# A two-block transformer layer on one core: GpSimd's tile arithmetic moved to VectorE, gates stored as tanh, and the modulation's products moved between stages

## The chip, the core and the metric

The program runs on one core of a Trainium2 chip. The time is the device time of one execution in microseconds (us), median over runs; the profile shows one such execution. The core's engines are named as in the profile: PE is TensorE's matmul queue, PEld its weight loads, DVE is VectorE, ACT ScalarE, POOL GpSimd, SP SyncE, which here issues the DMA transfers. Each engine runs its own instructions in order and waits for the others by semaphores.

## What is computed

256 tokens of width 2048 go through two blocks, all in float32. The first mixes by an S5 state space model and a gated DeltaNet, the second by sliding-window attention and gated linear attention (GLA); each ends in a gated convolutional FFN, and the second is modulated by a vector c. Cut to what the change touches:

```python
h = rmsnorm(x, mix_norm_w)
u, qkv, z, b_raw, a_raw, g_s5, g_dn = split(h @ w_in)
glu_a, glu_b = split(s5_branch(u) @ s5_glu_w)
br_s5 = glu_a * sigmoid(glu_b)
br_dn = deltanet_branch(qkv, z, b_raw, a_raw) @ dn_proj_w
x = x + (sigmoid(g_s5) * br_s5 + sigmoid(g_dn) * br_dn) @ w_out
h = rmsnorm(x, ffn_norm_w)
act, val = split(causal_dwconv(h @ ffn_up, ffn_conv_w))      # 3 taps
x = rmsnorm(x + (silu(act) * val) @ ffn_down, final_norm_w)
mod = silu(c) @ w_mod + b_mod                                # 2048 x 12288
sh1, sc1, g1, sh2, sc2, g2 = split(mod)
h = rms_norm(x) * (1 + sc1) + sh1
merged = sigmoid(g_a) * (attention(h) @ w_br_a) + sigmoid(g_b) * (gla(h) @ w_br_b)
x = x + g1 * rms_norm(merged @ w_out2)
x = x + g2 * rms_norm(conv_ffn(rms_norm(x) * (1 + sc2) + sh2))
```

## The kernel before

**Jobs and units.** Each product with a weight matrix is a job; they run in the order u, ba, q, k, v, z, gs, glu, gdn, dnp, wout, up1a, dw1a, up1b, dw1b, then qa, ka, va, gk, qb, kb, vb, og, ga, gb, wba, wbb, wout2, up2a, dw2a, up2b, dw2b. A job is cut into groups of output columns. Its weights come in chunks of 1 MB by SP's queue into three buffers `raw` (`fetch`). Half a chunk is a unit: ACT rounds it to `hi` (L413), and `split` subtracts, `lo = raw - hi`, by `tt` (L271): the low part, 128x1024, usually on DVE. Four pairs hi, lo can be alive. `run` then issues for each k-tile a matmul with hi over 512 columns (the two parts of the activations) and one with lo over 256 (L451, L452), or three for jobs whose result has tokens on the partitions (L457 to L459).

**The evacuation.** Two PSUM tiles `main` alternate. When a group's last k-tile is issued, a generator `ev_...` empties it, a step between two k-tiles of the next group: `halves` copies one half by ACT (L469) and adds on DVE (`ev<-main,evlo`). In up1a and up1b (`ev_up`) follow a product with R, the row of inverse norms, on POOL; a scaling by ACT (`tmp<-ev,pv`); four multiply-adds of the convolution on DVE (L278, 255 and 254 columns); Silu on ACT; the product of the two halves on POOL (`tmp<-tmp`); and its split by ACT and DVE (`act1a`). The gates gs, gdn, ga and gb are evacuated by a tanh and an addition on POOL (L275) and stored to DRAM until the branch outputs are merged.

**Background work.** S5, DeltaNet, attention and GLA are generators too, stepped beside the main products; S5 must be finished before glu begins, DeltaNet before dnp. Their small matmuls go to the tiles `bank`. A scheduler then fixes each engine's final order.

**What POOL does before.** The low part of every fourth unit in gs, glu, ga, gb, up1a and up1b, and of the first four of qa and up2a (`on_pool`); the products with R; the gates' additions; the merges; part of S5's, DeltaNet's, attention's and GLA's arithmetic; the first squares of x, which are summed on PE.

**The modulation.** w_mod's 96 chunks of 1 MB share the `raw` buffers. DVE multiplies each with silu(c) and sums along the row (L404, the GEMV). `plan` places one after every second or third chunk of the jobs that `MOD_EVERY` names (L333):

```python
if (ci >= 4 or nm != "up1a") and mods < 96 and since >= self.MOD_EVERY.get(nm, 1 << 30):
    self.units.append((len(self.chunks), None, 0, 0))
```

Of the kernel before, what the change touches and what calls it, by code (L numbers as in the profile page):

```python
# [13 lines left out]
P = 128  # L14
L = 256
# [27 lines left out]
def job_list():  # L43
    """Groups name the 128-column tiles of each packed matrix."""
# [75 lines left out]
def tile_columns(src, w):  # L120
    """The matrix [k, tiles * 128] that the groups index, from the reference's one."""
# [117 lines left out]
def pieces(v, n):  # L239
    """v as n floats of 12 bits each and one of the rest."""  # L240
# [9 lines left out]
# ------------------------------------------------------------------ kernel  # L250
# [6 lines left out]
class Kern:  # L257
# [11 lines left out]
    # ---- small wrappers  # L269
# [31 lines left out]
    # ---- background  # L301
# [55 lines left out]
    def fetch(self, upto, part=None):  # L357
        """Loads chunks up to one; with part, only the next so many columns of one."""
# [28 lines left out]
    POOL_EVERY = {"gs": 4, "glu": 4, "ga": 4, "gb": 4, "up1a": 4, "up1b": 4}  # L387

    def on_pool(self, u):
        """Whether GpSimd makes the low parts of a unit."""  # L390
        j = self.chunks[self.units[u][0]][0].name
        n = u - self.job_start[j]
        e = self.POOL_EVERY.get(j, 0)
        return j in ("qa", "up2a") and n < 4 or e and n % e == 1

    def split(self, upto):
        while self.split_at < min(upto, len(self.units)):
# [16 lines left out]
            eng = self.G if self.on_pool(u) else self.V  # L414
            self.tt(lo, r, hi.bitcast(F32), A.subtract, eng)
# [3 lines left out]
    def run(self, name, rhs, evac, ready=None):  # L419
        """rhs(k): the [128, 512] split tile of k; evac(g, psum) makes the generator that empties a group."""  # L420
# [44 lines left out]
    def halves(self, ps, nf=2, out=None):  # L465
        """The sum of a group's two halves, [128, nf, 256]."""
# [26 lines left out]
    def exp(self, out, x, n, t):  # L493
        """out = e ** x, to float32's accuracy; x is overwritten."""
# [13 lines left out]
    def turns(self, th, tmp, hi=None):  # L508
        """th (overwritten) in turns modulo 1 as a list [e] in [-.5, .5], or (hi, lo) with hi of 16 bits."""
# [29 lines left out]
    def token_rows(self, bank, col, acc, n=1):  # L539
        """Sums over partitions of acc [128, 256] into bank[:, col:col+2], a token on each partition."""  # L540
# [3 lines left out]
    def spread(self, bank, at, r, dg):  # L544
        """bank[:, at:at+256] = r (a token on each partition) along every row."""
# [5 lines left out]
    # ---- set-up  # L551
# [34 lines left out]
    def split_scaled(self, k, x, w):  # L586
        """xs[k] = the two parts of x * w (w a column)."""
# [4 lines left out]
    def split_into(self, dst, x, scale=1.0):  # L592
        """dst [128, 512] = the two parts of x * scale."""
# [7 lines left out]
    def rsqrt_mean(self, out, sums):  # L601
        """out [128, 2] = (mean of squares + eps) ** -0.5 from the sums of groups [128, 2, n]."""
# [5 lines left out]
    def row_scale(self, r):  # L608
        """self.R = r (a token on each partition, [128, 2]) along rows."""
# [4 lines left out]
    def square_sums(self, x, sums, quick=False):  # L614
        """sums [128, 2] = sums of squares of x [128, 2, n]; quick: by two engines."""
# [8 lines left out]
    def tiles(self, name, g):  # L624
        """The columns of a group."""
# [3 lines left out]
    def to_features(self, i, x):  # L629
        """Columns 256 i to 256 i + 255 of x [128 tokens, 2, n], a column on each partition."""  # L630
# [9 lines left out]
    # ---- block 1  # L640
    def block1(self):
# [9 lines left out]
        # the functions' table is loaded before the data is there  # L651
# [58 lines left out]
        self.run("gs", self.xrhs, lambda g, ps: self.ev_gate(self.d_gs, g, ps, 1.0))  # L710
# [4 lines left out]
        self.run("gdn", self.xrhs, lambda g, ps: self.ev_gate(self.d_gdn, g, ps, 2.0))  # L715
# [24 lines left out]
    def ev_u(self, g, ps):  # L740
        raw = self.halves(ps)
        yield
        if g == 0:
            # written first so that these loads come after the first weights
# [7 lines left out]
        self.tt(u, eo(raw), eo(self.rbc(2)), A.mult, self.G)  # L752
# [56 lines left out]
    def ev_glu(self, f, ps):  # L809
# [8 lines left out]
        self.tt(raw[:, 0], raw[:, 0], gl, A.mult, self.G)  # L818
# [11 lines left out]
    def ev_dnp(self, g, ps):  # L830
# [8 lines left out]
        yield  # L839
# [17 lines left out]
    # ---- the S5 branch  # L857
    def s5_task(self):
# [3 lines left out]
        # two steps of the recurrence at a time: x[2m+1] = a^2 x[2m-1] + (a B u[2m] + B u[2m+1])  # L862
# [79 lines left out]
        self.ts(c1, c1, -1.0, A.mult, 0.0, A.add, G)  # L942

        def cmul(o, o2, x, y, p, q, op, op2):
            """o = x p op y q, o2 = y p op2 x q."""
            self.tt(o, x, p, A.mult, G)
            self.tt(t3, y, q, A.mult)
            yield
            self.tt(o, o, t3, op, G)
            yield  # L950
            self.tt(o2, y, p, A.mult, G)
            self.tt(t3, x, q, A.mult)
            yield
            self.tt(o2, o2, t3, op2, G)
# [28 lines left out]
        def tables(j):  # L983
# [20 lines left out]
        for j in range(8):  # L1004
# [21 lines left out]
            self.tt(t1, t1, t2, A.add, G)  # L1026
# [875 lines left out]
```

## Time and profile before

| | |
|---|---|
| runs | 3260.02, 3258.59, 3263.13 us, median 3260.02 |
| profiled execution | span 3257.4 us; no separate time of it is given |
| front: u to gdn | 7.4 to 697.7 us |
| k, v | 146.8 to 211.3, 211.3 to 277.1 |
| wout | 743.0 to 835.6, 189 GB/s |
| up1a, up1b | 835.6 to 1113.6, 1241.6 to 1513.3 |
| og, ga, gb | from 1944.8, 2033.6, 2153.8, to 2259.3 |
| wba, wbb | 2259.3 to 2304.6, 2304.6 to 2393.4 |
| wout2 | 2393.4 to 2504.0, 190 GB/s |
| up2a, up2b | 2504.0 to 2751.6, 2875.1 to 3119.2 |

A stage begins with its job's first main matmul and ends with the next job's. In the row of a stage the busy time of PE, PEld, DVE, ACT and POOL stand in this order, then the granted clock of PE as a share of full speed, the busy share of the DMA engines and what they moved. In a row of a group stand line, engine, operation, output<-inputs, shapes and count, then its busy time in us, the mean duration of one in ns, and the engine's idle time just before, with what ended it. In a row of waits stands who waited for whom, the total in us, how often, and the longest.

### The profile page before, as it was taken

How to read it: one execution, taken by the hardware profiler on the slowest of the kernel's cores; microseconds unless marked ns; L12 is line 12 of the kernel's file. 1: busy time of each engine (PE TensorE's matmuls, PEld its weight loads, DVE VectorE, ACT ScalarE, POOL GpSimd, SP SyncE). 2: the span in 40 equal slices, each digit the busy share in tenths (PEclk: the TensorE clock that was granted, in tenths of full speed). 3: DMA queues.
4: the chain of work that ended last, by engine and by line, in shares of the span. 5: the costliest groups of instructions: out<-in, count | busy, mean ns of one | idle time of the engine just before them, and what ended most of it. 6: DMA issues, size and time to landing. Idle time of an engine off the chain costs nothing.

```text
span 3257.4 us, 46596 instructions
## 1 busy us (share of the span) xinstructions
PE 3099.1 (95%) x18220; PEld 2665.1 (82%) x18220; DVE 2300.3 (71%) x3043; ACT 1589.3 (49%) x2276; POOL 872.4 (27%) x491
## 2 busy tenths in 40 slices
PE   7889999999988999989989999999997999999998
PEld 6767789888877788777878898778887888898887
DVE  8999775666777767777667767887566666456655
ACT  4445543554444434444444544645444655445543
POOL 3665452231355403554020000332211111001101
PEclk9999999999999999999999999999998999999999
DMA  6334464665566677666756668666755555555553
GB/s 242 132 127 141 174 227 156 237 235 207 220 240 244 236 264 263 254 245 241 256 188 241 228 247 317 240 248 247 278 194 184 206 192 184 187 198 186 190 192 131
DMA packets 130829, 701.73 MB, mean 215 GB/s; under 512 B 20200, under 2 KB 33176, under 8 KB 53680
## 3 DMA queue, kind: packets, MB, share of 16 engines
q1 hardware_dynamic: 130608, 698.75, 60.0%
q8 instruction: 143, 2.34, 0.3%
q14 instruction: 78, 0.64, 0.1%
HBM read 674.26 MB, written 24.44 MB: 214 GB/s over the span
## 4 chain that ended last, share of the span: by engine, by line
PE 44%; DVE 3%; DMA 1%; issue 1%; ACT 1%; DVEq 0%; SPq 0%; ACTq 0%
PE main L451 19%; PE main L452 10%; PE main L457 5%; PE main L458 5%; PE main L459 5%; DMA raw<-in_wmod 1%; DVE lo L271 1%; DVE X L271 0%; PE bank L634 0%; DVE big L278 0%; ACT L282 0%; DVE raw L404 0%; DVE asm L275 0%; ACT X L282 0%; PE bank L1663 0%
## 5 line engine op out<-in xcount | busy, mean ns | idle before, releaser
L451 PE MATMUL main<-xs,hi 128*128 128x512 f32 x5440 | 1922.5, 396 | 17.2 <-ACT hi L413 9.2
L271 DVE TENSOR_TENSOR lo<-raw,hi 128x1024 fp32r<-128x1024 f32 x940 | 1201.3, 1282 | 628.7 <-ACT hi L413 626.1
L452 PE MATMUL main<-xs,lo 128*128 128x256 f32 x5440 | 1541.4, 284 | 56.4 <-DVE lo L271 38.7
L413 ACT CAST hi<-raw 128x1024 fp32r<-128x1024 f32 (+1 forms) x1024 | 1063.2, 1043 | 1000.7 <-PE main L451 560.5
L451 PEld LDWEIGHTS main<-xs,hi 128*128 128x128 f32 x5440 | 1030.5, 190 | 250.3 <-DVE xs L278 10.7
L452 PEld LDWEIGHTS main<-xs,lo 128*128 128x128 f32 x5440 | 1031.5, 190 | 83.6 <-DVE lo L271 49.8
L271 POOL TENSOR_TENSOR tmp<-tmp 128x256 f32<-128x256 f32 (+1 forms) x93 | 187.6, 2017 | 647.0 <-ACT tmp L282 646.6
L271 POOL TENSOR_TENSOR lo<-raw,hi 128x1024 fp32r<-128x1024 f32 x84 | 211.5, 2518 | 534.3 <-ACT hi L413 447.5
L404 DVE CUSTOM_DVE_ANT_0 raw<-raw,sc 128x2048 f32<-128x2048 f32 x96 | 242.4, 2525 | 42.2 <-DMA raw<-in_wmod 41.7
L271 POOL TENSOR_TENSOR ev<-ev,R 128x512 f32<-128x512 f32 x76 | 140.4, 1847 | 282.6 <-DVE ev L271 282.6
L278 DVE SCALAR_TENSOR_TENSOR tmp<-ev,pv,tmp 128x255 f32<-128x255 f32 (+1 forms) x352 | 162.7, 524 | 74.7 <-ACT tmp L282 74.7
L282 ACT ACTIVATE tmp<-ev,pv 128x256 f32<-128x256 f32 x176 | 88.1, 548 | 119.5 <-POOL ev L271 119.3
L271 DVE TENSOR_TENSOR ev<-main,evlo 128x512 f32<-128x512 f32 (+1 forms) x190 | 129.0, 679 | 14.3 <-ACT evlo L469 10.5
L457 PE MATMUL main<-hi,xs 128*128 128x256 f32 (+1 forms) x448 | 138.6, 309 | 0.0
L458 PE MATMUL main<-lo,xs 128*128 128x256 f32 (+1 forms) x448 | 137.4, 307 | 0.0
L459 PE MATMUL main<-hi,xs 128*128 128x256 f32 (+1 forms) x448 | 137.1, 306 | 0.0
L469 ACT COPY evlo<-main 128x512 f32<-128x512 f32 (+1 forms) x203 | 117.0, 576 | 13.7 <-PE main L452 13.7
L271 POOL TENSOR_TENSOR ev<-ev,tmp 128x512 f32<-128x512 f32 (+1 forms) x48 | 59.4, 1238 | 200.1 <-DVE ev L271 107.0
L451 PE MATMUL main<-ysp,hi 128*128 128x512 f32 x256 | 92.0, 400 | 0.4 <-DVE ev L271 0.4
L457 PEld LDWEIGHTS main<-hi,xs 128*128 128x128 f32 x448 | 84.1, 188 | 6.0 <-issue 1.7
L458 PEld LDWEIGHTS main<-lo,xs 128*128 128x128 f32 x448 | 84.3, 188 | 4.9 <-issue 0.7
L459 PEld LDWEIGHTS main<-hi,xs 128*128 128x128 f32 x448 | 84.5, 189 | 4.7
(336 smaller groups left out, 3863.0 us busy)
## 6 DMA issues: line engine op xcount, KB each, us to landing
raw<-in_w_in SPq DMA_DIRECT2D x164, 1024.0 KB, 4.9
raw<-in_wmod SPq DMA_DIRECT2D x96, 1024.0 KB, 5.1
raw<-in_ffn_up SPq DMA_DIRECT2D x88, 1024.0 KB, 5.0
raw<-in_w_up SPq DMA_DIRECT2D x88, 1024.0 KB, 4.8
raw<-in_ffn_down SPq DMA_DIRECT2D x38, 1024.0 KB, 5.0
raw<-in_w_down SPq DMA_DIRECT2D x38, 1024.0 KB, 4.8
raw<-in_w_out SPq DMA_DIRECT2D x32, 1024.0 KB, 4.8
raw<-in_s_glu_w SPq DMA_DIRECT2D x16, 1024.0 KB, 4.9
```

Of the source, the lines that this page charges most:

```text
L271: (eng or self.V).tensor_tensor(out=out, in0=a, in1=b, op=op)
L278: self.V.scalar_tensor_tensor(out=out, in0=a, scalar=s, in1=b, op0=op0, op1=op1)
L282: self.S.activation(out, a, f, bias=bias, scale=scale, **kw)
L404: self.V.tensor_tensor_reduce(r, r, self.sc, 1.0, 0.0, A.mult, A.add, self.mod[:, m:m + 1])
L413: self.S.copy(hi, r)
L451: T.matmul(cur[:, f, :], hi[:, s], x, start=first, stop=False)
L452: T.matmul(cur[:, f, 0:L], lo[:, s], x[:, 0:L], start=False, stop=last)
L457: T.matmul(cur[:, h, :w], xh, hi[:, s], start=first, stop=False)
L458: T.matmul(cur[:, h, :w], xh, lo[:, s], start=False, stop=False)
L459: T.matmul(cur[:, h, :w], xl, hi[:, s], start=False, stop=last)
L469: self.S.copy(lo[:, :nf], ps[:, :nf, L:])
```

## The change

All arithmetic on tiles leaves GpSimd. The low parts are all DVE's, `on_pool` and `POOL_EVERY` are gone, and every `tt` or `ts` that named GpSimd is now on DVE. The gates are stored as tanh, without the addition; whoever uses them computes (t + 1) * x in one instruction. The sums of the first squares come from a token-major copy of x, loaded at the start, by two squares with a sum on ACT. The GEMVs per job change from (up1a 20, dw1a 8, up1b 22, dw1b 8, qb 4, kb 4, vb 8, og 8, ga 8, gb 6) to (wout 5, up1a 4, dw1a 12, up1b 4, dw1b 12, qb 4, kb 4, vb 8, og 8, ga 8, gb 8, wba 4, wbb 8, wout2 7). The last three modulation vectors are formed after wout2.

```diff
-    MOD_EVERY = {"up1a": 2, "dw1a": 3, "up1b": 2, "dw1b": 3, "qb": 2, ... "wba": 2, "wbb": 2}
+    MOD_EVERY = {"wout": 2, "up1a": 11, "dw1a": 2, "up1b": 11, "dw1b": 2, "qb": 2, ... "wbb": 2, "wout2": 2}
-                if (ci >= 4 or nm != "up1a") and mods < 96 and ...
+                if (ci >= 6 or nm != "wout") and mods < 96 and ...
-    POOL_EVERY = {"gs": 4, "glu": 4, "ga": 4, "gb": 4, "up1a": 4, "up1b": 4}
-            eng = self.G if self.on_pool(u) else self.V
-            self.tt(lo, r, hi.bitcast(F32), A.subtract, eng)
+            self.tt(lo, r, hi.bitcast(F32), A.subtract)
...
-        for i in range(4):
-            self.tt(sq[:, i > 0], x[:, 4 * i:4 * i + 4], x[:, 4 * i:4 * i + 4], A.mult, G)
...
+        xt = self.ys32.rearrange("p (h n) -> p h n", h=2)
+        self.dma(xt, ap["xt"])
+        for h in range(2):
+            self.act(self.tmp[:, 0:2048], xt[:, h], AF.Square, accum=self.ss[0][:, h, 0:1])
...
     def ev_gate(self, dst, g, ps):
-        self.tt(raw, raw, self.rbc(2), A.mult, self.G)
+        self.tt(raw, raw, self.rbc(2), A.mult)
         self.act(raw, raw, AF.Tanh, scale=0.5)
-        self.ts(raw, raw, c, A.mult, c, A.add, self.G)
...
     def ev_dnp(self, g, ps):
-        self.tt(raw, raw, t[:, 0], A.mult, self.G)
-        self.tt(raw, raw, t[:, 1], A.add, self.G)
+        self.stt(raw, t[:, 0], 1.0, raw, A.add, A.mult)
+        self.stt(raw, raw, 2.0, t[:, 1], A.mult, A.add)
...
     def ev_up(self, b, f, i, act, done, ps):
-            self.tt(raw, raw, self.rbc(2), A.mult, self.G)
+            self.tt(raw, raw, self.rbc(2), A.mult)
...
-        self.tt(cv[:, 0], cv[:, 0], cv[:, 1], A.mult, self.G)
+        self.tt(cv[:, 0], cv[:, 0], cv[:, 1], A.mult)
...
+        self.run("wout2", self.xrhs, self.ev_wout2)
+        self.flush()
         sh2, sc2 = self.modulation(3), self.modulation(4)
         self.tt(gw2, self.modulation(5), self.pv("ffnpost", 0, 16), A.mult)
         self.stt(a2, sc2, 1.0, self.pv("ffnpre", 0, 16), A.add, A.mult)
-        self.run("wout2", self.xrhs, self.ev_wout2)
-        self.flush()
```

The same kind of edit, an engine left out of the call, is made in S5 (`cmul`, `roundn`, the sums of the scan), in DeltaNet, in attention's rotation, in GLA, in `ev_qkv`, `ev_z`, `ev_glu`, `ev_wba`, `ev_wbb`, `ev_down`, and in the residual additions after wout2 and at the end. POOL's queue falls from 359 instructions of the program's order to 15.

What the diff doesn't show is the order that results. DVE in the middle of up1a, one group of columns before:

```order
L271 TENSOR_TENSOR lo<-raw,hi 128x1024
L271 TENSOR_TENSOR ev<-main,evlo 128x512
L271 TENSOR_TENSOR lo<-raw,hi 128x1024
L278 SCALAR_TENSOR_TENSOR tmp<-ev,pv,tmp 128x255 x2
L278 SCALAR_TENSOR_TENSOR tmp<-ev,pv,tmp 128x254 x2
L271 TENSOR_TENSOR lo<-raw,hi 128x1024
L404 ISA raw,mod<-raw,sc 128x2048
L404 ISA mod 128x1
L271 TENSOR_TENSOR act1a<-tmp,act1a 128x256
```

and one group now:

```order
L271 TENSOR_TENSOR ev<-main,evlo 128x512
L271 TENSOR_TENSOR ev<-ev,R 128x512
L271 TENSOR_TENSOR lo<-raw,hi 128x1024
L278 SCALAR_TENSOR_TENSOR tmp<-ev,pv,tmp 128x255 x2
L278 SCALAR_TENSOR_TENSOR tmp<-ev,pv,tmp 128x254 x2
L271 TENSOR_TENSOR lo<-raw,hi 128x1024
L271 TENSOR_TENSOR tmp<-tmp 128x256
L271 TENSOR_TENSOR lo<-raw,hi 128x1024
L271 TENSOR_TENSOR act1a<-tmp,act1a 128x256
L271 TENSOR_TENSOR lo<-raw,hi 128x1024
```

Before, the evacuation's sum is followed by a low part and the multiply-adds, with the products by R and `tmp<-tmp` in POOL's queue and a GEMV in almost every group. Now both products stand in DVE's order, one low part stands between each two steps, and a GEMV stands in one group of five or six.

PE where S5's last matmuls (`bank`, L1053 and L1056, in the changed kernel L1029 and L1032) stand among the main products of gs, before:

```order
L451 MATMUL main<-xs,hi 128x512
L1053 MATMUL bank_66<-big,ysp 32x127 x4
L452 MATMUL main<-xs,lo 128x256
L451 MATMUL main<-xs,hi 128x512
L1053 MATMUL bank_66<-big,ysp 32x127 x4
L1056 MATMUL bank_66<-big,ysp 32x128 x16
L452 MATMUL main<-xs,lo 128x256
```

and now:

```order
L442 MATMUL main<-xs,lo 128x256
L441 MATMUL main<-xs,hi 128x512
L1029 MATMUL bank_66<-big,ysp 32x127 x4
L442 MATMUL main<-xs,lo 128x256
L1029 MATMUL bank_66<-big,ysp 32x127 x4
L1032 MATMUL bank_66<-big,ysp 32x128 x16
L441 MATMUL main<-xs,hi 128x512
```

Before, these rows come after 59 of the 512 main matmuls of gs; now after 448. S5 is spread over the stages q to gs, and DeltaNet's doubling levels, which stood among glu's products, stand among gdn's.

## Rows read from the trace of the kernel before

**Rows 1.** The page, part 1: busy time of each engine.

```profile
PE 3099.1 (95%) x18220; PEld 2665.1 (82%) x18220; DVE 2300.3 (71%) x3043; ACT 1589.3 (49%) x2276; POOL 872.4 (27%) x491
```

**Rows 2.** Waits in up1a: us in total, times, longest.

```profile
ACT act1a L282 <- POOL tmp L271: 60.6, 20, 4.0
...
ACT tmp L282 <- POOL ev L271: 53.8, 19, 3.7
...
DVE tmp L278 <- ACT tmp L282: 36.9, 20, 2.9
...
PE main L452 <- DVE lo L271: 12.8, 12, 1.6
```

**Rows 3.** Busy time by stage (window, length, engines, PEclk, DMA share, GB/s).

```profile
7.40:697.70 690.30, 643.94 (x4210) 540.11 (x4211) 548.37 (x875) 332.39 (x466) 294.98 (x182) 0.97 0.52 182
146.80:211.30 64.50, 58.90 (x434) 47.41 (x433) 61.07 (x112) 32.63 (x44) 39.13 (x21) 0.97 0.39 135
211.30:277.10 65.80, 60.27 (x434) 47.76 (x433) 64.20 (x109) 35.40 (x48) 39.75 (x20) 0.97 0.38 132
835.60:1113.60 278.00, 253.31 (x1418) 215.58 (x1417) 216.35 (x248) 130.22 (x194) 150.84 (x62) 1.00 0.65 242
1241.60:1513.30 271.70, 251.60 (x1410) 215.78 (x1409) 211.44 (x236) 129.89 (x188) 139.93 (x62) 0.99 0.69 251
1944.80:2033.60 88.80, 88.80 (x515) 78.19 (x514) 65.56 (x64) 41.22 (x47) 2.42 (x1) 1.00 0.83 309
2033.60:2153.80 120.20, 110.18 (x611) 92.38 (x610) 98.59 (x129) 70.21 (x108) 38.28 (x24) 0.97 0.68 249
2153.80:2259.30 105.50, 103.22 (x610) 89.24 (x609) 84.50 (x139) 56.20 (x90) 34.38 (x23) 1.00 0.65 221
2259.30:2304.60 45.30, 45.30 (x259) 39.33 (x258) 28.34 (x30) 21.66 (x27) 10.31 (x8) 1.00 0.88 331
2304.60:2393.40 88.80, 88.80 (x515) 78.20 (x514) 50.52 (x51) 42.09 (x54) 24.89 (x15) 1.00 0.71 242
2504.00:2751.60 247.60, 247.60 (x1431) 218.13 (x1430) 171.28 (x243) 146.32 (x214) 30.14 (x21) 1.00 0.55 194
2875.10:3119.20 244.10, 244.10 (x1411) 214.86 (x1410) 163.50 (x215) 137.22 (x194) 30.69 (x21) 1.00 0.55 192
```

**Rows 4.** DVE's groups by line, front (busy us, mean ns | idle before).

```profile
L271 DVE TENSOR_TENSOR lo<-raw,hi 128x1024 fp32r<-128x1024 f32 x165 | 221.2, 1345 | 89.2 <-ACT hi L413 88.8 <-issue 0.2
...
L278 DVE SCALAR_TENSOR_TENSOR big<-ev,pv,big 128x255 f32<-128x255 f32 x24 | 25.9, 1111 | 0.4 <-ACT big L282 0.4
...
L271 DVE TENSOR_TENSOR big<-big 128x512 f32<-128x512 f32 x24 | 15.9, 672 | 0.0
...
L278 DVE SCALAR_TENSOR_TENSOR xs<-big,pv,xs 128x256 fp32r<-128x256 f32 x14 | 15.4, 1153 | 0.6 <-ACT xs L282 0.6
```

**Rows 5.** The same view, og.

```profile
L271 DVE TENSOR_TENSOR lo<-raw,hi 128x1024 fp32r<-128x1024 f32 x32 | 39.1, 1223 | 21.1 <-ACT hi L413 21.1
...
L404 DVE CUSTOM_DVE_ANT_0 raw<-raw,sc 128x2048 f32<-128x2048 f32 x8 | 18.3, 2289 | 0.7 <-DMA raw<-in_wmod 0.6
```

**Rows 6.** The same view, up2a.

```profile
L278 DVE SCALAR_TENSOR_TENSOR tmp<-ev,pv,tmp 128x255 f32<-128x255 f32 x42 | 18.3, 477 | 0.0
...
L271 DVE TENSOR_TENSOR act2a<-tmp,act2a 128x256 fp32r<-128x256 f32 x21 | 8.9, 425 | 21.6 <-ACT act2a L282 21.6
```

**Rows 7.** POOL's groups by line and shape, front.

```profile
L271 POOL TENSOR_TENSOR ev<-ev,R 128x512 f32<-128x512 f32 x31 | 52.1, 1682 | 139.9 <-DVE ev L271 139.9
...
L271 POOL TENSOR_TENSOR lo<-raw,hi 128x1024 fp32r<-128x1024 f32 x16 | 39.6, 2478 | 42.5 <-ACT hi L413 38.2 <-DMA d_m<-ev 2.1 <-issue 1.2
...
L275 POOL TENSOR_SCALAR ev<-ev 128x512 f32<-128x512 f32 x15 | 12.3, 821 | 9.0 <-ACT ev L282 9.0
...
L271 POOL TENSOR_TENSOR tmp<-big 128x1024 f32<-128x1024 f32 x4 | 7.7, 1924 | 9.1 <-DMA big<-in_x 8.9
```

**Rows 8.** Waits of the whole run.

```profile
PE bank L634 <- DVE tmp L275: 28.1, 4, 17.3
```

More of the change, by code (lines that the diff above doesn't have):

```diff
@@ L330, in spawn @@
         return g
-    MOD_EVERY = {"up1a": 2, "dw1a": 3, "up1b": 2, "dw1b": 3, "qb": 2, "kb": 2, "vb": 2, "og": 2, "ga": 2, "gb": 2, "wba": 2, "wbb": 2}
+    MOD_EVERY = {"wout": 2, "up1a": 11, "dw1a": 2, "up1b": 11, "dw1b": 2, "qb": 2, "kb": 2, "vb": 2, "og": 2, "ga": 2, "gb": 2, "wba": 2, "wbb": 2, "wout2": 2}
     def plan(self, names):
@@ L343, in plan @@
                 since += 1
-                if (ci >= 4 or nm != "up1a") and mods < 96 and since >= self.MOD_EVERY.get(nm, 1 << 30):
+                if (ci >= 6 or nm != "wout") and mods < 96 and since >= self.MOD_EVERY.get(nm, 1 << 30):
                     self.units.append((len(self.chunks), None, 0, 0))
@@ L709, in block1 @@
         self.run("z", self.xrhs, self.ev_z)
-        self.run("gs", self.xrhs, lambda g, ps: self.ev_gate(self.d_gs, g, ps, 1.0))
+        self.run("gs", self.xrhs, lambda g, ps: self.ev_gate(self.d_gs, g, ps))
         while not self.s5_done:
@@ L714, in block1 @@
         self.run("glu", lambda k: self.ysp[:, k], self.ev_glu)
-        self.run("gdn", self.xrhs, lambda g, ps: self.ev_gate(self.d_gdn, g, ps, 2.0))
+        self.run("gdn", self.xrhs, lambda g, ps: self.ev_gate(self.d_gdn, g, ps))
         self.finish(mix, "dn")
@@ L817, in ev_glu @@
         yield
-        self.tt(raw[:, 0], raw[:, 0], gl, A.mult, self.G)
+        self.stt(raw[:, 0], gl, 1.0, raw[:, 0], A.add, A.mult)
         yield
@@ L1025, in s5_task @@
                 yield
-            self.tt(t1, t1, t2, A.add, G)
-            self.tt(t3, t3, t4, A.subtract, G)
+            self.tt(t1, t1, t2, A.add)
+            self.tt(t3, t3, t4, A.subtract)
             yield
@@ L1164, in dn_task @@
             ends = lambda t: t.rearrange("p (b n) -> p b n", n=P)[:, 0:3:2]
-            self.tt(k[:, h], k[:, h], r[:, 768:1024], A.mult, G)
-            self.tt(q[:, h], q[:, h], r[:, 1024:1280], A.mult, G)
-            self.tt(ends(at), ends(r[:, 0:384]), tri.unsqueeze(1).to_broadcast([P, 2, P]), A.add, G)
+            self.tt(k[:, h], k[:, h], r[:, 768:1024], A.mult)
+            self.tt(q[:, h], q[:, h], r[:, 1024:1280], A.mult)
+            self.tt(ends(at), ends(r[:, 0:384]), tri.unsqueeze(1).to_broadcast([P, 2, P]), A.add)
             yield
@@ L1444, in residual @@
                     x = self.x[:, h, c:c + 512]
-                    self.ts(x, x, sm[:, 4 + h:5 + h], A.mult, 0.0, A.add, G)
+                    self.ts(x, x, sm[:, 4 + h:5 + h], A.mult)
                     self.dma(d_x[:, h, c:c + 512], x)
@@ L1513, in block2 @@
                 x, y = x1[:, h, c], self.x[:, h, c]
-                if h and i in (1, 2):
-                    self.ts(y, y, r1[:, 1:2], A.mult, 0.0, A.add, G)
-                    self.tt(x, x, y, A.add, G)
-                else:
-                    self.stt(x, y, r1[:, h:h + 1], x, A.mult, A.add)
+                self.stt(x, y, r1[:, h:h + 1], x, A.mult, A.add)
             self.square_sums(x1[:, :, c], self.ss[1][:, :, i], i == 3)
@@ L1532, in block2 @@
                 x, o = self.x[:, h, c], x2[:, h, c]
-                if h and i < 2:
-                    self.act(x, x, AF.Copy, scale=r1[:, 1:2])
-                    self.tt(o, o, x, A.add, G)
-                else:
-                    self.stt(o, x, r1[:, h:h + 1], o, A.mult, A.add)
+                self.stt(o, x, r1[:, h:h + 1], o, A.mult, A.add)
                 self.dma(ap["out"][:, h, c], o)
@@ L1574, in ev_gate2 @@
         yield
-        self.ts(raw, raw, 1.0, A.mult, 1.0, A.add, self.G)
-        yield
-        yield
         self.dma(dst[g], raw)
@@ L1593, in ev_wba @@
         yield
-        self.tt(raw, raw, t[:, 0], A.mult, self.G)
-        yield
+        self.stt(raw, t[:, 0], 1.0, raw, A.add, A.mult)
         yield
@@ L1604, in ev_wbb @@
         yield
-        self.tt(raw, raw, t[:, 0], A.mult, self.G)
+        self.stt(raw, t[:, 0], 1.0, raw, A.add, A.mult)
         yield
-        self.tt(self.merged[:, 2 * g:2 * g + 2], raw, t[:, 1], A.add, self.G)
+        self.tt(self.merged[:, 2 * g:2 * g + 2], raw, t[:, 1], A.add)
     def ev_wout2(self, g, ps):
@@ L1823, in gla_task @@
                 yield
[L1824 removed]
+            self.tt(sq[0], sq[0], sq[1], A.add)
             yield
             yield
[L1827 removed]
+            self.tt(sq[0][:, 0:L], sq[0][:, 0:L], sq[0][:, L:], A.add)
             yield
```

62 lines of the change are left out of this document (19 added, 43 removed).

## The prediction

> **What bounds the kernel now.** I read the page's engine totals first, then the waits of one wide stage, then the table by stage, and last the costliest groups of VectorE (DVE) and GpSimd (POOL). TensorE (PE) is busy for 95% of the span, DVE for 71%, POOL for 27% [rows 1]. So the kernel is bound by TensorE on average, and a change that removes POOL's arithmetic can win time only where PE waits. It does wait in one of the long stages: in up1a, PE is held up by the low parts that DVE makes (12.8 us in 12 waits), and behind these stand the waits that the change touches: ScalarE (ACT) waits 60.6 us for POOL's product, 53.8 us for POOL's multiplication by R, and DVE waits 36.9 us for ACT [rows 2]. The reader is to see a chain there: DVE to POOL to ACT to DVE to ACT to POOL to ACT to DVE, once per group of columns, on engines that run in order.
>
> The table by stage says what PE loses. up2b computes the same product as up1a and up1b, without R and without the modulation's transfers, and takes 244.1 us with PE busy all through; up1a takes 278.0 and up1b 271.7 [rows 3]. og, with DVE busy 65.56 of 88.80 us, also keeps PE full. In k and v, DVE is busy 61.07 of 64.50 us (94.7%) and 64.20 of 65.80 (97.6%): there DVE is the bound, though DVE over the whole front (u to gdn, 7.4 to 697.7) is busy only 548.37 of 690.30 [rows 3].
>
> **The change part by part.** All sums are against the profiled span of 3257.4 us; the median of the three runs, 3260.02, stands 2.6 above it, and I add that at the end.
>
> *What a DVE instruction costs with and without POOL beside it.* A low part takes 1345 ns in the front, where POOL is busy 43% of the time, and 1223 in og, where POOL runs one instruction [rows 4, 5]. The 255-column multiply-adds take 1111 in the front and 477 in up2a, and the 14 listed splits of the input 1153; the GEMV takes 2289 in og [rows 4 to 6]. So in the front alone, 165 x 0.122 + 24 x 0.634 + 14 x 0.676 (477 taken for a split, too) = 20.1 + 15.2 + 9.5 = 45 us of DVE's time go away if POOL's presence is the cause. The Trainium skill ("SBUF — State Buffer", section "Who interferes with whom") says more: the port pair that the two engines share is an exclusive lock, whoever comes second is blocked for the other's whole instruction. The trace shows a mean lengthening of a tenth for the low parts, so less than that rule would make of POOL's 43%; by the rule the relief would be larger than 45 and the outcome nearer my second case.
>
> *Front.* POOL is busy 294.98 us there [rows 3]. The first squares' four products (7.7) and the gates' 15 additions (12.3) go away [rows 7]; the rest, 275, moves to DVE. A 512-column product costs 1682 ns on POOL and 672 on DVE [rows 4, 7], a ratio of 0.40, so 110 us arrive (a low part, 2478 against 1223, has 0.49; the squares' sums, which go too, are left in to make up for it). DVE: 548.4 - 45 + 110 = 613 us. The change in order spreads this work: S5's last matmuls stood in the first of the eight groups of gs, now at the seventh's end, so DVE's peak in q to z spreads over gs, and DeltaNet's levels move from glu to gdn, where DVE has room. At v's share, 613 / 0.976 = 628, the front gains 62; at k's share, 647, it gains 43. I take **56**, nearer v's, since only three groups' relief was counted. Ends: no relief at all, 658 / 0.976 = 674, gains 16; DVE without a gap, 613, gains 77. The token-major copy of x, 2.1 MB, is paid in the start: at wbb's 242 GB/s [rows 3] it is 9 us of transfer while PE still waits for its inputs; I count it at nothing, covered by the fact that R is first needed when the first group is evacuated. Uncovered it costs 9, and the lower end has room for it.
>
> *up1a and up1b.* One of 22 groups costs DVE now 216.35 / 22 = 9.83 busy and (278.0 - 216.35) / 22 = 2.80 idle. After: four low parts 4 x 1.223 = 4.89 (POOL's one comes back), the evacuation's sum and the R product 2 x 0.672 = 1.34, four multiply-adds 1.91, the product and the last low part 2 x 0.425 = 0.85, and the GEMVs, four per job instead of 20 or 22, 4 x 2.289 / 22 = 0.42 [rows 4 to 6]. Sum **9.41**, 85% of up2b's 11.10 per group. The order puts one low part between each two steps of the chain, 1.22 us in which ACT does its step. So PE should bound these stages, and at most 278.0 + 271.7 - 2 x 244.1 = 61.5 comes back. up2a, with DVE at 69%, still takes 3.5 more than up2b [rows 3]; I take 7 off for that and 2.5 for waits that remain: **52**. If the 2.80 of idle time stays, a group takes 12.21 and the two jobs 537, a gain of 13.
>
> *The GEMVs that arrive elsewhere.* dw1a and dw1b get 12 each instead of 8: a down job streams 23.1 MB and then 12.6 in 88.8 x 22/16 = 122 us, 293 GB/s, less than the 309 that og sustained without a wait [rows 3]. I give these **+2** for the up jobs' leftovers at their start (-5 to 8). wba and wbb get 4 and 8, and wba already moves 331 GB/s at 88% of the DMA engines: 15.0 MB + 4.2 in 45.3 us would be 424 GB/s, more than 331 / 0.88 = 376, so 51 us; wbb would need 337, about what wba sustains. **-5** (0 to -12). gb (8 for 6) moves 221 GB/s [rows 3], wout (5) and wout2 (7) less by the table of stages: nothing.
>
> *ga, gb.* PE is idle 10.0 and 2.3 us in them [rows 3]; the gates' addition and store go earlier by POOL's step, the low parts come back to DVE (98.59 of 120.2 busy). **+10** (0 to 20, the rest being matmuls stretched by waits).
>
> *Ends of stages.* PE waits 28.1 us in four places for DVE's rows at a block's turn [rows 8]; DVE does these beside POOL's scaling. **+3.5**, an eighth (-3 to 10). Against it: the first four low parts of qa and up2a are DVE's again, 4 x 1.22 = 4.9 each where PE waits; **-2** and **-4**. Three modulation vectors are now formed after wout2's flush: **-1**.
>
> Sum: 56 + 52 + 2 + 10 + 3.5 - 5 - 2 - 4 - 1 = 111.5. Span 3145.9, time **3148**.
>
> **The rivals.**
> *Larger (0.17).* DVE has no gap in the front (77), PE bounds up1 fully (61.5), ga and gb give 20, the ends 10, dw1 2, and nothing is lost: 170, so 3090. For it: og and up2b show PE never waiting with DVE at 74 and 67%. Against: DVE reaches 85% in up1.
>
> *The waits stay (0.18).* DVE's long instructions have another cause than POOL, or its queue, now the longer by 110 us in the front, holds the low parts back. Front 16, up1 13, the rest as above (+3.5): 33, so 3227. For it: DVE in k and v has no room. The Trainium skill ("Perfetto Trace Analysis", section "Optimizing Scalar/DVE Operations") speaks against this change in the same way: where DVE is saturated, offloading some work from it to other engines, even GpSimd, may make sense. By that rule k and v are the place where taking POOL's help away costs most; the rows bear it out in these jobs and not in up1, where DVE is idle 22%.
>
> *Slower (0.07).* DVE runs in order, and in up1 two of POOL's steps now stand in its queue: each waits for ACT at DVE's head, where before POOL waited. If one more such wait of 36.9 / 20 = 1.85 us [rows 2] comes to each group, it takes 9.41 + 2.80 + 1.85 = 14.06, the 44 groups 619 instead of 549.7, a loss of 69; with the front's 16 and the rest's 3.5 the time is 3309. It decides from about 4.3 us of idle time per group, 13.8 in all, where up1's loss eats the front's 56 and the 3.5. Against: the low part of 1.22 us between each two steps.
>
> That the change doesn't do what it says can be excluded: GpSimd's queue falls to a handful of instructions. What it may do is something less; that is the second rival.
>
> **How the numbers follow.** The forecast's own case has 0.58. Within 0.2%, 6.5 us, is about what a measurement of this kernel tells from no change. The waits-stay case is faster in 0.16 and the same in 0.02; the slower case slower in 0.06 and the same in 0.01. Faster 0.58 + 0.17 + 0.16 = 0.91, same 0.03, slower 0.06. The range goes from the larger case's 3090 less 5 for its uncertainty, 3085, up to 3215, which a front of 16 beside an up1 of 52 (3188), or an up1 of 13 with a front of 56 (3187), stay within, and of the waits-stay case the lighter half; some 16 in 100 lie above or below.
>
> **What would show it.** Low parts at about 1.23 us everywhere, the 255-column multiply-adds near 0.48, the GEMV near 2.3. up1a and up1b at 247 to 252 us, DVE busy near 207 in each. The front from 690 to about 634, with DVE at 95% or more of q to gs. wba longer by some 5 us. DVE's waits for ACT in up1 at under 1 us per group. The prediction is wrong if low parts stay at 1.35 (another cause), or if DVE in up1 is idle 2.8 us a group or more with PE waiting for low parts behind it.

## The result and the profile after

The changed kernel takes 3113.35 us, median of four runs (3109.70 to 3119.41), beside 3259.56 for the kernel before: a ratio of 0.9549, 95% interval 0.9536 to 0.9563. It is 146 us faster; 112 were forecast, and the time lies inside the range of 3085 to 3215. The profiled execution's span is 3109.3 us, 148.1 less than that of [rows 1].

The page, part 1, of the changed kernel:

```profile
PE 3055.0 (98%) x18216; PEld 2650.4 (85%) x18216; DVE 2314.6 (74%) x3479; ACT 1591.9 (51%) x2275; POOL 3.0 (0%) x11
```

POOL's 872 us have gone, and DVE, which took over the work (all but the first squares and the gates' additions, which were dropped or went to other engines), is busy for only 14 us more than before. This is the main reading of the case: what POOL's instructions had cost DVE was nearly as much as what they had saved it. The single durations give an estimate of both: against the median of their kind in the changed kernel, DVE's instructions had been too long by some 254 us in sum, and the work that DVE gained is some 312 us.

Busy time by stage, the changed kernel: front, up1a, up1b, ga, wba, wbb, with columns as in [rows 3]:

```profile
7.70:634.10 626.40, 624.41 (x4206) 530.25 (x4207) 533.28 (x1027) 333.58 (x467) 1.70 (x5) 1.00 0.58 204
772.10:1017.00 244.90, 244.90 (x1418) 215.64 (x1417) 197.04 (x286) 135.46 (x200) 0.00 (x0) 1.00 0.58 211
1140.50:1384.60 244.10, 244.10 (x1411) 214.85 (x1410) 194.86 (x269) 133.55 (x193) 0.00 (x0) 1.00 0.59 214
1898.10:2001.30 103.20, 101.71 (x586) 87.25 (x585) 85.16 (x129) 66.18 (x97) 0.00 (x0) 1.00 0.75 273
2106.80:2154.20 47.40, 46.17 (x263) 39.55 (x261) 37.16 (x61) 20.64 (x29) 0.00 (x0) 1.00 0.92 347
2154.20:2249.70 95.50, 91.24 (x513) 79.51 (x513) 76.99 (x86) 43.67 (x56) 0.00 (x0) 0.98 0.88 339
```

Against [rows 3] the front is 63.9 us shorter, up1a 33.1, up1b 27.6, ga 17.0; wba is 2.1 longer and wbb 6.7. PE is busy for all but 2 us of the front and all through both up jobs.

DVE's groups in the front, the changed kernel, answering to [rows 4]:

```profile
L271 DVE TENSOR_TENSOR lo<-raw,hi 128x1024 fp32r<-128x1024 f32 x181 | 220.5, 1219 | 53.3 <-ACT hi L404 52.8
...
L278 DVE SCALAR_TENSOR_TENSOR big<-ev,pv,big 128x255 f32<-128x255 f32 x24 | 10.9, 478 | 0.0
...
L278 DVE SCALAR_TENSOR_TENSOR xs<-big,pv,xs 128x256 fp32r<-128x256 f32 x14 | 5.9, 477 | 0.0
```

The low part falls from 1345 to 1219 ns, the multiply-add from 1111 to 478, the split from 1153 to 477. The tile's own view tells how the mean had come about; it gives the shortest, median and longest duration in ns over the whole run, before:

```profile
L271 DVE TENSOR_TENSOR lo<-raw,hi x940: 683/1225/3384, 7.4 to 3233.7; 128x1024 fp32r<-128x1024 f32 x185, 128x512 fp32r<-128x512 f32 x3
```

and after:

```profile
L271 DVE TENSOR_TENSOR lo<-raw,hi x1024: 682/1224/1237, 7.7 to 3087.1; 128x1024 fp32r<-128x1024 f32 x171
```

The median did not move. Some low parts had taken up to 3.4 us, and none takes more than 1.24 now: DVE was held up at single instructions, not slowed throughout.

### The profile page after: what moved, and what is told of

Read it like the earlier page. It is cut to its first block, busy times and chain, and to the rows that moved or that the text cites. A ratio compares the mean times of both kernels' runs of the same rounds, so it can differ in the third digit from the quotient of the medians.

```text
span 3109.3 us, 46298 instructions
## 1 busy us (share of the span) xinstructions
PE 3055.0 (98%) x18216; PEld 2650.4 (85%) x18216; DVE 2314.6 (74%) x3479; ACT 1591.9 (51%) x2275; POOL 3.0 (0%) x11
## 4 chain that ended last, share of the span: by engine, by line
PE 95%; DVE 2%; DMA 2%; issue 1%; ACT 0%; SPq 0%; DVEq 0%; ACTq 0%
PE main L441 43%; PE main L442 22%; PE main L447 8%; PE main L449 8%; PE main L448 8%; DMA raw<-in_w_branch_gla 1%; DVE lo L271 1%; PE bank L994 1%; DMA ysp<-in_xt 0%; DMA raw<-in_wmod 0%; PE bank L1209 0%; PE bank L624 0%; PE bank L1029 0%; PE bank L1203 0%; ACT tmp L282 0%
## 5 line engine op out<-in xcount | busy, mean ns | idle before, releaser
L271 DVE TENSOR_TENSOR lo<-raw,hi 128x1024 fp32r<-128x1024 f32 (+1 forms) x1024 | 1245.2, 1218 | 642.4 <-ACT hi L404 638.7
L442 PEld LDWEIGHTS main<-xs,lo 128*128 128x128 f32 x5440 | 1024.8, 188 | 12.8 <-DVE lo L271 5.3
L395 DVE CUSTOM_DVE_ANT_0 raw<-raw,sc 128x2048 f32<-128x2048 f32 x96 | 219.6, 2287 | 49.1 <-DMA raw<-in_wmod 48.7
L278 DVE SCALAR_TENSOR_TENSOR tmp<-ev,pv,tmp 128x255 f32<-128x255 f32 (+1 forms) x352 | 146.2, 477 | 0.0
L449 PE MATMUL main<-hi,act1a 128*128 128x512 f32 (+1 forms) x220 | 76.9, 349 | 0.0
L449 PE MATMUL main<-hi,act2a 128*128 128x512 f32 (+1 forms) x220 | 76.9, 349 | 0.0
L449 PE MATMUL main<-hi,act2b 128*128 128x512 f32 (+1 forms) x220 | 76.9, 349 | 0.0
L449 PE MATMUL main<-hi,act1b 128*128 128x512 f32 (+1 forms) x220 | 76.9, 349 | 0.0
```

Source lines behind the costliest of these rows:

```text
L271: (eng or self.V).tensor_tensor(out=out, in0=a, in1=b, op=op)
L278: self.V.scalar_tensor_tensor(out=out, in0=a, scalar=s, in1=b, op0=op0, op1=op1)
L395: self.V.tensor_tensor_reduce(r, r, self.sc, 1.0, 0.0, A.mult, A.add, self.mod[:, m:m + 1])
L442: T.matmul(cur[:, f, 0:L], lo[:, s], x[:, 0:L], start=False, stop=last)
L449: T.matmul(cur[:, h, :w], xl, hi[:, s], start=False, stop=last)
```

## The experiments

The theories. *Contention*: POOL's instructions lengthen DVE's. *Handoffs*: POOL's slow steps, at which other engines wait in order, hold the low parts back. *Load*: the GEMVs left the up jobs, where DVE had no room. The stages of up1a and up1b tell them apart.

**1. The GEMVs where they were.** The changed kernel with the old table (the last three modulation vectors stay behind wout2):

```diff
-    MOD_EVERY = {"wout": 2, "up1a": 11, "dw1a": 2, ...}
+    MOD_EVERY = {"up1a": 2, "dw1a": 3, ...}
-                if (ci >= 6 or nm != "wout") and ...
+                if (ci >= 4 or nm != "up1a") and ...
```

> The changed kernel with the GEMVs where they were before (up1a 20, up1b 22, dw1 8 and 8, none in wba, wbb, wout2). If the move of the GEMVs made the gain in up1 (theory: load), up1a and up1b go back to some 278 and 272 us, and only wba and wbb get their 9 us back: about 3165. If POOL's contention and its handoffs made it, one group of up1a has 4.89 + 1.34 + 1.91 + 0.85 + 20/22 x 2.29 = 11.1 us of DVE against 11.1 of PE: up1a and up1b at 250 to 258, the total 3115 to 3135.

Measured 3107.75 us, ratio to the kernel before 0.9531 (0.9515 to 0.9546). up1a with its 21 GEMVs in the window:

```profile
775.70:1020.70 245.00, 245.00 (x1419) 215.75 (x1418) 226.12 (x316) 136.39 (x199) 0.00 (x0) 1.00 0.78 279
```

DVE is busy for 92% and PE never waits. So load alone is not the cause: without POOL, up1 has room for the GEMVs. Both theories' totals missed, on the pessimistic side: even the 5 to 13 us more in each up job did not come.

**2. The new GEMV table alone.** The kernel before with the changed kernel's table, and the last three modulation vectors after wout2; POOL as it was.

> The kernel before with the GEMVs of the changed one (and the last three modulation vectors after wout2), POOL as it was. Load: up1a and up1b at 245 to 250 us, the total about 3260 - 55 + 9 = 3214. Handoffs or contention: DVE's waits for ACT stay at 1.5 us and more per group and up1a stays over 258; total 3235 or more.

Measured 3219.55, ratio 0.9876 (0.9861 to 0.9890): 40 us faster than before. up1a:

```profile
835.00:1085.90 250.90, 247.57 (x1418) 216.91 (x1417) 178.37 (x217) 131.46 (x197) 123.35 (x62) 0.99 0.57 205
```

So nearly the same edit is worth 40 us on the old kernel and costs 6 us on the new one (10 when it is measured again in experiment 8). It and POOL's removal buy the same thing, room on DVE, and their gains do not add. The load theory's numbers for up1 came nearly true here, and DVE still waits 30.5 us for ACT in up1a (36.9 before): the waits that were expected to keep up1a over 258 stayed, and PE is fed all the same.

**3. The chain's two products back on POOL**, in the changed kernel, in up1a and up1b only:

```diff
-            self.tt(raw, raw, self.rbc(2), A.mult)
+            self.tt(raw, raw, self.rbc(2), A.mult, self.G)
+            yield
...
-        self.tt(cv[:, 0], cv[:, 0], cv[:, 1], A.mult)
+        self.tt(cv[:, 0], cv[:, 0], cv[:, 1], A.mult, self.G if b == "1" else None)
```

> The changed kernel with the product by R and the product of the two halves of up1a and up1b back on POOL, nothing else on it. Handoffs: DVE waits for ACT some 1.8 us per group again and PE for low parts; up1a and up1b at 255 or more. Contention alone: the 255-column multiply-adds at 0.6 to 0.7 us and the low parts near 1.3, DVE's busy time about the same 9.3 per group (1.1 less, 0.9 more), so up1a at 245 to 248. The other stages as in the changed kernel: total 3113 to 3120, or 3135 and more with handoffs.

Measured 3115.43, ratio 0.9557 (0.9539 to 0.9575). up1a takes 245.0:

```profile
771.80:1016.80 245.00, 245.00 (x1419) 215.74 (x1418) 180.19 (x241) 135.56 (x198) 71.81 (x42) 1.00 0.59 208
```

DVE does wait behind POOL's two products:

```profile
DVE act1a L271 <- ACT act1a L282: 21.7, 20, 1.1
DVE tmp L278 <- ACT tmp L282: 10.4, 6, 1.7
```

So handoffs through POOL cost DVE 32 us and PE nothing here, where DVE is busy 74% of the stage. Of contention's signs the low parts came (1309 ns) and the multiply-adds did not (476, for 600 to 700 expected). That is not yet the end of the handoffs: the ninth experiment fills DVE up.

**4. POOL reads whose results nobody uses.** The changed kernel; in `split`, after the low part:

```diff
+            nm = self.chunks[c][0].name
+            n = {"up1a": u % 2, "up1b": 2, "q": 1, "k": 1, "v": 1, "z": 1}.get(nm, 0)
+            h = hi.bitcast(F32)
+            for _ in range(n):
+                self.tt(self.idle, h[:, 0:512], h[:, 512:1024], A.mult, self.G)
```

> The changed kernel; POOL in addition multiplies the halves of hi, 128x512, into a tile nobody reads: once per unit in q, k, v, z, once in two units in up1a, twice per unit in up1b, never in other jobs; nobody waits for it. Contention: low parts in up1b at 1.4 us or more, in up1a at 1.28 to 1.35, the front's q to z 10 to 30 us longer, up1b over 250. Handoffs alone: every stage as in the changed kernel within 1 us, low parts at 1.22.

Measured 3270.36, ratio 1.0036 (1.0023 to 1.0049): this alone takes the whole gain back. Windows of q to z, of up1a and of up1b:

```profile
67.20:315.80 248.60, 222.27 (x1456) 185.51 (x1457) 247.85 (x358) 111.22 (x148) 121.98 (x62) 0.93 0.41 143
```

```profile
820.90:1065.90 245.00, 245.00 (x1419) 215.74 (x1418) 224.54 (x284) 137.91 (x200) 98.07 (x43) 1.00 0.60 208
1189.40:1545.80 356.40, 279.97 (x1409) 233.91 (x1409) 351.16 (x265) 129.34 (x192) 303.99 (x174) 0.91 0.41 145
```

In the changed kernel q to z take 203.6 us with DVE busy 196.3; here 248.6, DVE busy all of it: 45 us longer, where 10 to 30 were expected. In up1a the dose lengthens DVE by 27.5 us (197.0 to 224.5) and PE still covers it; in up1b DVE becomes the bound and the stage takes 356.4 instead of 244.1. PE waits so often that its granted clock falls from 1.00 to 0.93 and 0.91 in the two lengthened stretches, but there it is not the bound. The groups of DVE there, with the evacuation's sum, and the waits:

```profile
L271 DVE TENSOR_TENSOR lo<-raw,hi 128x1024 fp32r<-128x1024 f32 x88 | 172.3, 1958 | 4.5 <-ACT hi L404 4.5
L278 DVE SCALAR_TENSOR_TENSOR tmp<-ev,pv,tmp 128x255 f32<-128x255 f32 x42 | 57.7, 1412 | 0.0
...
L271 DVE TENSOR_TENSOR ev<-ev,R 128x512 f32<-128x512 f32 x21 | 24.9, 1187 | 0.6
...
L271 DVE TENSOR_TENSOR ev<-main,evlo 128x512 f32<-128x512 f32 x21 | 14.2, 678 | 0.0
```

```profile
PE main L447 <- DVE lo L271: 76.0, 41, 4.8
...
ACT hi L404 <- POOL idle L271: 4.5, 2, 2.4
```

Nobody uses what POOL makes. ACT waits 4.5 us here (13.2 in q to z) until POOL has read a `hi` that is to be overwritten, and DVE is busy for 351 of the 356 us, so the longer stage is the work of contention. It is selective: the sum that reads one operand from PSUM (`main`) stays at 678 ns, while the product with R, of the same size and with both operands in SBUF, takes 1187 (690 in up1a of the changed kernel). DVE's and POOL's timelines there (start, duration in us) show the stops:

```profile
1269.95 1.21 DVE L271 TENSOR_TENSOR lo<-raw,hi 128x1024 fp32r<-128x1024 f32 x1
...
1271.44 2.29 DVE L271 TENSOR_TENSOR lo<-raw,hi 128x1024 fp32r<-128x1024 f32 x1
1273.65 0.68 DVE L271 TENSOR_TENSOR ev<-main,evlo 128x512 f32<-128x512 f32 x1
1274.37 1.07 DVE L271 TENSOR_TENSOR ev<-ev,R 128x512 f32<-128x512 f32 x1
1275.36 2.31 DVE L271 TENSOR_TENSOR lo<-raw,hi 128x1024 fp32r<-128x1024 f32 x1
```

```profile
1269.74 2.91 POOL L271 TENSOR_TENSOR idle<-hi 128x512 f32<-128x512 f32 x1 [2.26 <-ACT hi L404]
...
1272.73 2.16 POOL L271 TENSOR_TENSOR idle<-hi 128x512 f32<-128x512 f32 x1
```

The two engines stop each other in turn. The first low part takes its usual 1.21 us, and POOL's product beside it 2.91, with 1.3 the shortest of its kind in this stage. The next low part starts at 1271.44, while that product runs until 1272.65; it ends 1.08 us after it, at 1273.73, and has taken 2.29. POOL's second product ends 1.16 us after that low part. The sum from PSUM beside it is untouched.

**5. Only the low parts off POOL**, in the kernel before:

```diff
-    POOL_EVERY = {"gs": 4, "glu": 4, "ga": 4, "gb": 4, "up1a": 4, "up1b": 4}
+    POOL_EVERY = {}
-        return j in ("qa", "up2a") and n < 4 or e and n % e == 1
+        return False
```

> The kernel before with every low part on DVE; all other work stays on POOL. If the price is POOL's slow low parts (84 of 2.5 us that PE waits for), up1a and up1b fall by half their excess to some 262, and ga and gb by 10; total 3210 to 3225. If it is contention with the rest of POOL's arithmetic, DVE gets 21 x 1.25 = 26 us more in up1a and is blocked as before: up1a at 275 or more, total 3250 to 3275.

Measured 3231.34, ratio 0.9912 (0.9897 to 0.9927), between the two expectations. up1a:

```profile
840.10:1109.20 269.10, 252.60 (x1418) 215.64 (x1417) 207.31 (x270) 130.55 (x195) 112.25 (x41) 1.00 0.68 249
```

DVE's low parts in up1a, before and here:

```profile
L271 DVE TENSOR_TENSOR lo<-raw,hi 128x1024 fp32r<-128x1024 f32 x65 | 87.8, 1358 | 6.3 <-ACT hi L413 6.2
```

```profile
L271 DVE TENSOR_TENSOR lo<-raw,hi 128x1024 fp32r<-128x1024 f32 x87 | 108.5, 1263 | 13.6 <-ACT hi L413 13.6
```

DVE makes 22 more low parts and is busy 9 us less than in [rows 3]; its GEMVs fall from 2808 to 2284 ns and its 255-column multiply-adds from 686 to 482. So in up1a it was POOL's low parts that lengthened DVE's instructions, and little of that is left here. ga falls from 120.2 to 104.9: nearly all of its gain was the low parts. But up1a keeps 25 us of its excess, with 62 us of idle time on DVE: there the lengthening of DVE's instructions is the smaller part of the price. The ninth experiment, whose up1a has the same work on each engine, shows the larger one.

**6. The first squares on POOL**, as before, in the changed kernel: the loads of `xt` and ACT's squares replaced by the loop that the diff removes.

> The changed kernel with the first squares made and summed as before (POOL, then PE). Contention in the start: the input's splits at 1.1 us each again, u at 60 to 63 us instead of 50 to 54, the total 3121 to 3127. If the 2 MB more of loads cost as much as the squares did, u stays within 2 us.

Measured 3121.75, ratio 0.9583 (0.9567 to 0.9599), 8 us slower than the changed kernel; u takes 61.3 us instead of 50.0 (50.0 to 54.1 in the profiles of the kernels that share the changed start). The splits of the input, with POOL's squares beside them:

```profile
L278 DVE SCALAR_TENSOR_TENSOR xs<-big,pv,xs 128x256 fp32r<-128x256 f32 x16 | 15.8, 1041 | 3.7 <-ACT xs L282 3.7
```

They are back at 1041 ns (477 in the changed kernel), and PE waits 6.8 us for them. Part of the 11 us is clock: with PE idle more often, u is granted 0.89 of full speed, as before the change, instead of 1.00, and PE's busy time there is 53.27 us instead of 48.54. The 2 MB of loads and ACT's squares cost less than POOL's squares did.

**7. POOL instructions that only write, and with one input.** The changed kernel, in up1a twice a memset per unit, paced by a copy of one column of hi, in up1b twice a product of hi with 1; nobody uses the results.

> The changed kernel; POOL twice per unit, with nobody waiting: in up1a it only writes (a 128x512 memset, after a copy of one column that sets its pace), in up1b it multiplies 128x512 of hi by 1 (one input). If a POOL instruction that only writes blocks nobody, up1a stays at 245 with low parts at 1.22; if any access blocks, low parts are at 1.4 or more. With one input read the block should be as long as the instruction: low parts in up1b at 1.5 or more, up1b over 250.

Measured 3115.47, ratio 0.9559 (0.9545 to 0.9573). In up1a, POOL's groups and DVE's low parts:

```profile
L410 POOL COPY idle<-hi 128x1 f32<-128x1 f32 x85 | 95.1, 1119 | 42.0 <-ACT hi L404 41.8
L412 POOL MEMSET idle<- 128x512 f32 x172 | 90.6, 527 | 10.0
```

```profile
L271 DVE TENSOR_TENSOR lo<-raw,hi 128x1024 fp32r<-128x1024 f32 x88 | 107.7, 1224 | 46.3 <-ACT hi L404 46.3
```

and the low parts in up1b:

```profile
L271 DVE TENSOR_TENSOR lo<-raw,hi 128x1024 fp32r<-128x1024 f32 x87 | 127.3, 1463 | 7.6 <-ACT hi L404 7.6
```

91 us of memsets leave the low part at 1224: writing blocks nobody. One input read does block (1463). The copy of a single column takes 1119 ns: it comes just behind a low part's start and is itself stopped until that ends, as one pair shows:

```profile
901.28 1.23 DVE L271 TENSOR_TENSOR lo<-raw,hi 128x1024 fp32r<-128x1024 f32 x1 [1.22 <-ACT hi L404]
```

```profile
901.38 1.17 POOL L410 COPY idle<-hi 128x1 f32<-128x1 f32 x1 [0.44 <-ACT hi L404]
```

ACT waits 52 us in up1a until POOL is done with `hi`, and the stage still takes 245.0. up1b takes 246.7, less than expected: DVE is busy for 238.7 of it and just fits.

**8. The first experiment again.**

> The first experiment's kernel again, for its interval against the changed kernel's 3113: without GEMVs in wba, wbb and wout2 these stages take 45.5, 88.7 and 108.0, and no other stage differs by over 1.5 us, so 6 to 10 us less, 3103 to 3108. If the first measurement was chance, 3111 to 3116.

Measured 3103.25, ratio 0.9521 (0.9507 to 0.9535), clear of the changed kernel's interval by a hair, and 10 us faster by the medians; all eight times of this kernel, here and in experiment 1 (3101.76 to 3109.30), lie below the changed kernel's lowest. The windows of wba and wbb, with no GEMV in them:

```profile
2107.30:2153.10 45.80, 45.80 (x264) 39.85 (x263) 31.94 (x40) 22.66 (x30) 0.00 (x0) 1.00 0.86 318
2153.10:2241.80 88.70, 88.70 (x514) 78.07 (x513) 56.83 (x66) 42.16 (x54) 0.00 (x0) 1.00 0.68 245
```

They are 8.4 us shorter than in the changed kernel. This is the fastest of all versions: without POOL, the GEMVs stand better in the up jobs, where they had been.

**9. Experiments 1 and 3 together**: the old table, and the chain's products on POOL.

> The first and the third experiment together: GEMVs where they were (20 and 22 in the up jobs), and the two products of up1a's and up1b's chain on POOL, low parts and all else on DVE. DVE's busy time in up1a would be the third experiment's 180 and 15 more GEMVs, 180 + 15 x 2.3 = 215 of 245. If a handoff's price is DVE's idle time at its queue's head, about 2 us per group that nothing fills once DVE is this full, up1a takes 255 to 270. If busy time alone decides, 245 to 247, total 3106 to 3112.

Measured 3162.40, ratio 0.9692 (0.9676 to 0.9708). up1a:

```profile
773.80:1043.50 269.70, 252.65 (x1418) 215.67 (x1417) 208.25 (x270) 130.32 (x195) 109.79 (x41) 1.00 0.69 248
```

Either edit alone leaves up1a at 245; both make it 269.7. The low parts are at 1258 ns, less than in experiment 3 (1309), so it is not the length of DVE's instructions. DVE's waits for what comes through POOL are:

```profile
DVE tmp L278 <- ACT tmp L282: 29.7, 18, 1.7
...
DVE act1a L271 <- ACT act1a L282: 16.1, 15, 1.1
```

They are 45.8 us, 32.1 in experiment 3, and with the 208.25 that DVE is busy they exceed the 245 that PE needs. The second product on POOL is:

```profile
L271 POOL TENSOR_TENSOR tmp<-tmp 128x256 f32<-128x256 f32 x20 | 67.4, 3372 | 54.5 <-ACT tmp L282 54.5
```

It takes 3372 ns, against 1953 in the third experiment, where few GEMVs run; the product with R takes 2068, against 1630. One group's timeline, DVE, POOL, ACT:

```profile
904.50 1.22 DVE L271 TENSOR_TENSOR lo<-raw,hi 128x1024 fp32r<-128x1024 f32 x1
905.63 2.29 DVE L395 CUSTOM_DVE_ANT_0 raw<-raw,sc 128x2048 f32<-128x2048 f32 x1
...
909.01 0.42 DVE L271 TENSOR_TENSOR act1a<-tmp,act1a 128x256 fp32r<-128x256 f32 x1 [1.08 <-ACT act1a L282]
```

```profile
904.78 3.75 POOL L271 TENSOR_TENSOR tmp<-tmp 128x256 f32<-128x256 f32 x1 [2.44 <-ACT tmp L282]
```

```profile
908.56 0.42 ACT L282 ACTIVATE act1a<-tmp 128x256 fp32r<-128x256 f32 x1 [3.86 <-POOL tmp L271]
```

DVE had the low part running when POOL's product began, then the GEMV; POOL ends 0.6 us after the GEMV (908.53 against 907.92), ACT starts at once, and DVE, in order, stands idle for ACT for 1.08 us, as long as it does without a GEMV in experiment 3. So the GEMV does not fill that wait: DVE stops POOL, and then waits for what it stopped. The wait that grows, from 10.4 to 29.7 us, is the one at the multiply-adds, behind the product with R. That up1a would stay at 245 if DVE did not stop POOL is argued, not tried alone. DVE's idle time per group is (269.7 - 208.3) / 22 = 2.79 us, the 2.80 of the kernel before.

## Why the prediction was right

By its own steps, forecast beside the profiled stages (gain in us):

| step | forecast | measured |
|---|---|---|
| front | 56 (16 to 77) | 63.9 |
| up1a, up1b | 52 (13 to 61.5) | 33.1 + 27.6 = 60.7 |
| dw1 2, ends 3.5, vectors -1 | 4.5 | 11.0 (dw1a 4.5, dw1b 6.5), wout2 2.6 |
| ga, gb | 10 | 17.0 + 0.0 |
| wba, wbb | -5 | -8.8 |
| first low parts of qa, up2a | -6 | -0.8, +0.2 |

They sum to 145.8 of 148.1 us. The time is 35 us below the forecast because four steps came out 7 to 9 us above their number each, and the charge for qa and up2a, 5 us, did not come. At 3113 it lies nearer the larger rival (3090) than the forecast (3148).

*The cause was right, its size was not.* The relief of DVE was put at 45 us in the front, from three groups. DVE's work there came out at 533 us, not 613: if the 110 that was estimated did arrive, that is 548 + 110 - 533 = 125 us of relief; the single durations, taken as above, give some 101. The sentence "only three groups' relief was counted" saw this coming and put no number to it. With that, the front's bound was named wrong: it is not DVE (85% busy) but PE (624.41 of 626.40), and DVE's share of q to gs is 93%, where 95 or more was to show the forecast right. That the front came near its 56 is therefore partly luck: by the forecast's own rule, 533 us at v's share, it would have gained 144, and PE's own time ends the gain at 63.9. Experiment 4 shows the cause by itself: 61 POOL instructions whose results nobody uses lengthen q to z by 45 us.

*The lock.* From the means I held that the trace shows less than the Trainium skill's rule would make. That was the misreading of a mean. In experiment 4 single instructions stand still until POOL's ends, and POOL's until theirs, a sum with one operand in PSUM is exempt, and in experiment 7 writes without a read block nobody. The Trainium skill ("SBUF — State Buffer", section "Who interferes with whom") says the same of DVE instructions with two SBUF inputs, POOL instructions that read SBUF, and that the order of issue decides who blocks. The mean was small before because most low parts were not lengthened at all: their median over the whole run is 1225, with 3384 the longest.

*up1.* DVE's 9.41 us per group came out at 197.04 / 22 = 8.96, and PE bounds the stage as argued, with no remainder of waits; the 9.5 us taken off for one were not needed. But the step that put the fewer GEMVs into this gain was not the reason for it: with the GEMVs back (experiment 1) up1a is still 245.0. Before, three things came together: contention on DVE, POOL's slow products at which DVE waited in order, and the GEMVs, which both filled DVE and stopped POOL. Taking away the GEMVs (250.9), or POOL's part (245.0), frees the stage; taking only the low parts from POOL (269.1) doesn't, and neither does leaving only the chain there (269.7), which in up1a is the same work on the same engines. So of the 33 us, the low parts on POOL were worth 9, and 24 hung on its two products beside the GEMVs. The prediction read PE's 12.8 us behind DVE's low parts and left out 9.6 us, in 11 waits, behind POOL's.

*The GEMVs elsewhere* cost 8.8 us in wba and wbb, 5 forecast, but not where it was forecast. wba was charged with 5.7 and pays 2.1, and in experiment 6, with the same GEMVs, nothing (45.3); wbb, for which nothing was charged, pays 6.7. Transfers are the cause: at 347 and 339 GB/s and about 0.9 of the DMA engines, ACT waits 22.4 us there for weights, and without the GEMVs (experiments 1 and 8) the stages take 45.8 and 88.7. So this part of the change is a loss that the rest covers. The start, counted at nothing, gained: u is 13 us shorter, and experiment 6 ascribes 7 to 11 of them to the squares. For qa and up2a the charge was wrong: their first low parts cost under 1 us.

*The rivals.* The waits did not stay, and in the front and the up jobs no DVE queue held PE up. k and v, where DVE had no room, became shorter, 51.7 and 51.0 us, with POOL's help gone (some of S5's work had left them, as the order showed), and q to z got longer when POOL was made busy again. The Trainium skill ("Perfetto Trace Analysis", section "Optimizing Scalar/DVE Operations") says that help for a saturated DVE, even GpSimd's, may make sense, as the second rival quotes it; the next sentence there warns that the two engines share a port, so that moving work between them might not help. These runs agree with the warning. dw1b and wout2, 6.5 and 2.6 us shorter, gained by POOL's removal and not by the GEMVs' new places: with the old places and no POOL (experiment 1) they take 135.4 and 108.0, as in the changed kernel, and with the new places and POOL (experiment 2) 141.3 and 110.7, as before.

## What to carry to other kernels

Before work is given to GpSimd, compare the shortest, median and longest duration of VectorE's two-input instructions in stages with and without it: the price stands in their durations, on whichever engine came second, and a list of waits does not show it, since the engine that is stopped counts as busy. A step handed to a slower engine was free here while the receiver had slack (74% busy) and cost 25 us of 245 when it was nearly full, so try it at both loads. And when such contention is removed, choose again what had been balanced under it: here the GEMVs' place, worth 40 us before, cost 6 to 10 after.

## What was not expected of the hardware

A POOL copy of one column, 128x1, took 1119 ns on average beside a running low part, where one like it in the kernel before took 187: it is stopped for the rest of the other's instruction, however little it reads itself. And VectorE stops GpSimd too: a low part and a 2.29 us GEMV in the way made POOL's 128x256 product 3.75 us long, where the shortest in that run took 0.75.
